# The last two attention heads' blocks in turns, and three orders tied around the end of the last QKV slab

## The chip, the cores and the metric

The kernel runs on one NeuronCore of a Trainium2 chip. The metric is the device time of one execution in microseconds, the median of repeated runs. Five engines work side by side, each through its own queue in order: PE (TensorE) multiplies into PSUM, DVE (VectorE), ACT (ScalarE) and POOL (GpSimd) work elementwise, and SP (SyncE) issues most DMAs. Line numbers (L823) are those of the kernel before.

## The reference

A decoder trunk of two layers on 512 tokens of width 1024, all in float32. Layer 0 has a convolution module, layer 1 differential attention; each is followed by a SwiGLU FFN and a gated input embedding. The change touches layer 1 alone, from its QKV product to its output product:

```python
qkv = x @ w_qkv                              # 1024 x 3072
q, k = rms_norm(q), rms_norm(k)              # per head, two components of 64
for each block of 128 queries, 8 heads, 2 components:
    probs = softmax(q @ k.T + bias, causal)
    w = probs[0] - lam * probs[1]
    o = w @ v                                # v 128 wide per head
o = rms_norm(o) * (1 - lambda_init)
h = h + o.reshape(S, 1024) @ w_o
...
h = h + sigmoid(rms_norm(h) @ ple_w_gate) * (p @ ple_w_proj)   # after the FFN
```

## The kernel before, in words

**Products.** A float32 product is three passes (`mm3`, L158 to L160): each operand is split into a high and a low part. A weight arrives by a DMA on SP's queue (`wraw`, two buffers), ACT copies its high part (L151), DVE subtracts the low part (L153; POOL does one split in each slab but the first).

**QKV in slabs.** Six slabs of 512 columns follow each other (`QKV`): q and k of heads 0 and 1, v of heads 0 to 3, q and k of heads 2/3, of 4/5, v of heads 4 to 7, q and k of heads 6/7. A slab has four token blocks (`tokens`), each a chain of 24 passes on PE. For a q/k slab, `unit` then copies the product to `q`, squares it on ACT, reduces it on DVE (L765), takes the power on POOL (L766, L767), scales on POOL (L769); `unit_end` transposes on PE (L775) and splits into the parts that the scores use: ACT (L783, L784), POOL (L788), DVE (L791, L793).

**Attention blocks.** A block is a head and 128 queries, (hd, qb), hd and qb from 0. `stage_s` makes two scores on PE (L820, L821; 128 to 512 keys wide by qb), reduces each against the bias on DVE (L823), takes the exponential on ACT (L827) and combines both on DVE (L830 to L832). `stage_t`, two blocks later, transposes on PE (L840) and copies on ACT (L842). `stage_a`, four blocks later, multiplies by v on PE (L853), and when a head is full scales it (L861, L871 to L876). `stage_o` transposes a finished head on PE (L883) and splits it (L182 on ACT, L183 on DVE). Scores have two PSUM buffers (`sc`), transposes two (`tp`).

**Their order.** `todo` lists the 32 blocks by head. The last number of each entry of `QKV` says how many blocks' stages are traced between the products of each token block, so 25 of the 32 blocks go into the slabs. What is left is taken one piece at a time by `step()`: first in `project`, the eight products with `ple_w_proj` that the gate needs at the end of the layer (48 passes, weights `pw`), then in `linear` with W_o. W_o's first two columns of tiles (m = 0, 1) run together, k by k, each k needing one finished head. The trace order is not the queue order: a scheduler places each instruction in its engine's queue by simulated times; `tc.issue_after(ins)` ties an instruction behind another one of its engine.

Of the kernel before, what the change touches and what calls it, by code (L numbers as in the profile page):

```python
# [24 lines left out]
NH = 8  # L25
# [47 lines left out]
HALVES = slice(0, DH), slice(DH, P)  # L73
LT = 2
LA = 4
SQ_ACT = True
PACK = True
E1 = True
GLO = 1
QKV = (("q", 0, (0, 0, 0, 0)), ("v", 0, (1, 1, 1, 2)), ("q", 1, (1, 1, 1, 2)), ("q", 2, (1, 1, 2, 1)), ("v", 1, (1, 1, 2, 2)), ("q", 3, (1, 1, 1, 1)))  # L80


@with_exitstack
def trunk(ctx, tc, xT, pT, wts, diag, dww, vec, rel, onehot, lamv, out):
# [9 lines left out]
    def sb(shape, tag, bufs, dt=F32):  # L94
        uid[0] += 1
        return pool.tile(shape, dt, tag=tag, name=f"{tag}_{uid[0]}", bufs=bufs)
# [65 lines left out]
    def wpart(w, k):  # L162
        return tuple(t[:, k * P : (k + 1) * P] for t in w)
# [115 lines left out]

    last_product = [None]  # L280

    def project(ph, m, w, o, step=lambda: None):

        acc = mm()
        for k in range(2):
            last_product[0] = mm3(acc, wpart(w, 2 * (m % 4) + k), ph[k], k == 0, k == 1)
            step()
        last_copy[0] = A.copy(o, acc)
        return o
# [457 lines left out]
    def unit(pair, ws, tb, between):  # L747

        if tb == 0:
            qk[pair] = [sb([P, 2, S], f"C{i}", 2, F32R) for i in range(6)]  # L750

            for c in range(2):
                with tc.issue_after(n2.last.ins):
                    G.memset(f(qk[pair][4 + c][HALVES[1 - c]]), 0.0)
        acc, r = tokens(ws, tb, between)
        q = big()
        A.activation(q, acc, AF.Copy, scale=r)
        sq = wk()
        if SQ_ACT:
            A.activation(sq, acc, AF.Square, scale=r)  # L760
        else:
            G.tensor_tensor(sq, q, q, ALU.mult)

        rs = sb([P, P // 2], "r8", 2)[:, :8]
        V.tensor_reduce(out=rs, in_=sq.rearrange("p (g d) -> p g d", g=8), op=ALU.add, axis=AX.X)  # L765
        G.tensor_tensor(rs, rs, meps, ALU.add)  # L766
        G.tensor_tensor(rs, rs, mhalf, ALU.pow)  # L767
        q3 = q.rearrange("p (g d) -> p g d", g=8)
        G.tensor_tensor(q3, q3, rs.unsqueeze(2).to_broadcast([P, 8, DH]), ALU.mult)  # L769
        return pair, tb, q  # L770

    def unit_end(pair, tb, q):
        t = tp()
        for i in range(4):
            T.transpose(t[:, i * P : (i + 1) * P], q[:, i * P : (i + 1) * P], ident)  # L775
        t4 = t.rearrange("p (h c t) -> p h c t", h=2, c=2)
        cut = slice(tb * P, (tb + 1) * P)
        qs, ks, kl = qk[pair][0:2], qk[pair][2:4], qk[pair][4:6]

        qg, kg = col("q_g"), gains[:, 0:1]  # L780
        for c in range(2):
            own, other = HALVES[c], HALVES[1 - c]
            A.activation(qs[c][own, :, cut], t4[own, :, 0], AF.Copy, scale=qg[own])  # L783
            A.activation(ks[c][own, :, cut], t4[own, :, 1], AF.Copy, scale=kg[own])  # L784
            if KDUP == "A":
                A.activation(ks[c][other, :, cut], t4[own, :, 1], AF.Copy, scale=kg[own])
            else:
                G.tensor_copy(ks[c][other, :, cut], f(ks[c][own, :, cut]))  # L788
        for c in range(2):
            own, other = HALVES[c], HALVES[1 - c]  # L790
            V.scalar_tensor_tensor(  # L791
                qs[c][other, :, cut], t4[own, :, 0], qg[own], f(qs[c][own, :, cut]), ALU.mult, ALU.subtract)
            V.scalar_tensor_tensor(  # L793
                kl[c][own, :, cut], t4[own, :, 1], kg[own], f(ks[c][own, :, cut]), ALU.mult, ALU.subtract)

    biases = {}
    stats = {}
    state = {}

    def stage_s(hd, qb):  # L800
        if qb == 0:
            biases[hd] = bias(hd)
        b = biases[hd]
        n = (qb + 1) * P
        brev = bass.AP(b.tensor, b.offset + (S - 1) - (S - n), [list(b.ap[0]), [-1, n]])
        qs, ks, kl = qk[hd // 2][0:2], qk[hd // 2][2:4], qk[hd // 2][4:6]
        i = hd % 2
        if qb == 0:
            stats[hd] = sb([P, 4, 6], "st", 2)
        es, st = [], stats[hd][:, qb]  # L810
        for c in range(2):
            cut = slice(qb * P, (qb + 1) * P)
            if not PACK or n > S // 2:
                acc = sc()
            elif c == 0:
                both = sc()
                acc = both[:, : S // 2]
            else:
                acc = both[:, S // 2 :]
            T.matmul(acc[:, :n], qs[c][:, i, cut], ks[c][:, i, 0:n], start=True, stop=False)  # L820
            T.matmul(acc[:, :n], qs[c][:, i, cut], kl[c][:, i, 0:n], start=False, stop=True)  # L821
            e = sb([P, S], ("acc", "rb")[qb % 2], 1) if c and E1 else big()
            V.tensor_tensor_reduce(  # L823
                out=e[:, :n], in0=acc[:, :n], in1=brev, scale=-1.0, scalar=3.0e38,
                op0=ALU.add, op1=ALU.min, accum_out=st[:, c : c + 1],
            )
            A.activation(e[:, :n], e[:, :n], AF.Exp, scale=-1.0, bias=st[:, c : c + 1], accum_out=st[:, 2 + c : 3 + c])  # L827
            es.append(e)

        V.reciprocal(st[:, 4:5], st[:, 3:4])  # L830
        V.scalar_tensor_tensor(st[:, 5:6], st[:, 4:5], mlam, st[:, 2:3], ALU.mult, ALU.mult)
        V.scalar_tensor_tensor(es[0][:, :n], es[1][:, :n], st[:, 5:6], es[0][:, :n], ALU.mult, ALU.add)  # L832
        state[hd, qb] = es[0]

    def stage_t(hd, qb):
        w_ = state[hd, qb]
        n = (qb + 1) * P
        t = tp()
        for k in range(qb + 1):
            T.transpose(t[:, k * P : (k + 1) * P], w_[:, k * P : (k + 1) * P], ident)  # L840
        wt_ = sb([P, S], ("wth", "wtl")[qb % 2], 2)
        A.copy(wt_[:, :n], t[:, :n])  # L842
        state[hd, qb] = wt_

    oacc = {}
    osb = {}

    def stage_a(hd, qb):
        if qb == 0:
            oacc[hd] = mm()  # L850
        own = slice(qb * P, (qb + 1) * P)
        for k in range(qb + 1):
            T.matmul(  # L853
                oacc[hd][:, own], state[hd, qb][:, k * P : (k + 1) * P],
                val[hd // 4, k // 2][:, k % 2, (hd % 4) * P : (hd % 4 + 1) * P], start=(k == 0), stop=(k == qb),
            )
        if qb % 2 == 1:
            if qb == 1:
                osb[hd] = sb([P, S], f"D{hd % 6}", 1)
            two = slice((qb - 1) * P, (qb + 1) * P)  # L860
            V.tensor_copy(osb[hd][:, two], oacc[hd][:, two])  # L861
        if qb == 3:
            o_ = osb[hd]

            rs = sb([P, P // 2], "r8", 2)[:, :8]
            e0 = sb([P, 4], "r0", 1)
            A.activation(e0, stats[hd][:, :, 2], AF.Square, scale=math.sqrt(P * EPS))
            sq = wk()
            for k in range(4):
                cut = slice(k * P, (k + 1) * P)  # L870
                A.activation(sq[:, cut], o_[:, cut], AF.Square, accum_out=rs[:, k : k + 1])  # L871
            G.tensor_tensor(rs[:, 0:4], rs[:, 0:4], e0, ALU.add)
            G.tensor_tensor(rs[:, 0:4], rs[:, 0:4], mhalf[:, 0:4], ALU.pow)
            rs = rs[:, 0:4]
            o3 = o_.rearrange("p (g d) -> p g d", g=4)
            G.tensor_tensor(o3, o3, rs.unsqueeze(2).to_broadcast([P, 4, P]), ALU.mult)  # L876

    ot = {}

# [7 lines left out]
        ot[hd] = (hi, lo)  # L887


    todo = [(hd, qb) for hd in range(NH) for qb in range(4)]  # L890
    stages = []
    for n in range(len(todo) + LA):
        for stage, at in ((stage_s, n), (stage_a, n - LA), (stage_t, n - LT)):
# [13 lines left out]
    for what, at, pace in QKV:  # L907
        ws = slab(GLO if at > 0 else 0)
        for tb in range(4):
# [10 lines left out]
            if (what, at, tb) == ("q", 0, 1):  # L920
                ph = pfeatures(1, [both(sb([P, 2, S], t, 1, F32R)) for t in ("B4", "B5")])
            elif (what, at, tb) == ("q", 0, 2):
                pw = [weight(parts=("B6", "B7"))]
    unit_end(*waiting)
    pw.append(weight())


    done = [0]
# [1 line left out]
    def step():  # L930
        if stages:
            n, s = stages.pop(0)
            s()
        else:
            n = 99
        while done[0] < NH and (n - LA - 3) // 4 > done[0]:
            stage_o(done[0])
            done[0] += 1

    pp = []  # L940
    for m in range(NC):
        if m % 2 == 0:
            o2 = sb([P, 2, S], f"C{m // 2 + 2}", 2)
        step()
        pp.append(project(ph, m, pw[m // 4], o2[:, m % 2], step))

    def heads_until(k):
        while done[0] <= k:
# [5 lines left out]
        V.tensor_tensor(h[m], acc, h[m], ALU.add)  # L954
        norm.chunk(m)

    linear(NC, ot, add_attn, 2, heads_until, step, parts={4: ("B0", "B1"), 5: ("B2", "B3")})
    n2 = Norm("ple_g1")
    ffn(norm, n2)

# [133 lines left out]
```

## Time and profile before

| | |
|---|---|
| median of 3 runs | 1285.97 us (1285.86 to 1286.89) |
| the profiled execution, its own time | 1286.35 us |
| its span | 1284.6 us |
| granted PE clock, mean | 0.999 |
| the last q/k slab and what follows to W_o's second pair of tiles | about 757 to 850 us of the span |

The span is what the trace shows; 1.75 us of the profiled execution's own time lie outside it. Times in the views are microseconds from the span's start.

### The profile page before, as it was taken

Reading aid. Unit: us, or ns where it says so; the run is one execution under the profiler, and the core shown is the slowest. Engines: PE = TensorE matmul, PEld = TensorE weight load, DVE = VectorE, ACT = ScalarE, POOL = GpSimd, SP = SyncE. Lnnn points to the kernel's source line nnn. Section 1 sums busy time; section 2 is a strip of 40 time slices with the busy share of each in tenths; the row PEclk is TensorE's granted clock in tenths of the full one; section 3 lists DMA queues with packets and bytes.
Section 4 is the critical chain, followed back from the end, with each engine's and each line's share of the span. In section 5 each row is a group of like instructions: output and inputs, shape, how many; then the busy total and the mean of one; then the engine's idle time right before and its main releaser. Section 6 shows DMA issues by size and latency. Waiting matters only on the chain.

```text
span 1284.6 us, 15478 instructions
## 1 busy us (share of the span) xinstructions
PE 1267.4 (99%) x5960; PEld 1051.5 (82%) x5960; DVE 707.2 (55%) x1040; ACT 523.3 (41%) x874; POOL 247.4 (19%) x223
## 2 busy tenths in 40 slices
PE   9999999999999999999999998999999999999998
PEld 8888688888888888888888887878888888888887
DVE  4897765543344434456677777536443344334445
ACT  5752464332222223254567768635321223222332
POOL 1754432000000000042346546131000000000030
PEclk9999999999999999999999999999999999999999
DMA  7555214223333333233342222022332222232231
GB/s 269 198 179 179 83 52 126 88 96 99 98 98 98 99 93 94 67 126 99 97 128 77 74 83 75 33 82 82 99 98 98 98 98 92 91 97 91 91 115 66
DMA packets 46838, 131.97 MB, mean 103 GB/s; under 512 B 5379, under 2 KB 9987, under 8 KB 46764
## 3 DMA queue, kind: packets, MB, share of 16 engines
q1 hardware_dynamic: 44640, 127.55, 31.1%
q10 hardware_dynamic: 2124, 3.43, 0.9%
q8 instruction: 47, 0.77, 0.3%
q14 instruction: 27, 0.22, 0.1%
HBM read 126.75 MB, written 4.21 MB: 102 GB/s over the span
## 4 chain that ended last, share of the span: by engine, by line
PE 81%; DVE 7%; DMA 4%; issue 3%; POOL 2%; ACT 2%; SPq 0%; ACTq 0%; DVEq 0%; POOLq 0%
PE mm L158 26%; PE mm L159 26%; PE mm L160 26%; DVE sc L421 2%; DVE wlo L153 2%; POOL wk L409 1%; DMA wraw<-in_wts 1%; PE mm L853 1%; ACT whi L151 1%; DMA po<-big 1%; PE sc L821 1%; PE sc L820 1%; PE tp L840 1%; DMA B<-po 0%; ACT A L182 0%
## 5 line engine op out<-in xcount | busy, mean ns | idle before, releaser
L151 ACT CAST whi<-wraw 128x1024 fp32r<-128x1024 f32 (+2 forms) x210 | 214.2, 1026 | 549.3 <-PE mm L160 356.4
L158 PE MATMUL mm<-A,wlo 128*128 128x512 f32 (+1 forms) x1080 | 420.8, 390 | 1.8 <-ACT A L182 1.8
L159 PE MATMUL mm<-A,whi 128*128 128x512 f32 (+1 forms) x1080 | 419.2, 388 | 0.0
L160 PE MATMUL mm<-A,whi 128*128 128x512 f32 (+1 forms) x1080 | 415.8, 389 | 0.0
L153 DVE TENSOR_TENSOR wlo<-wraw,whi 128x1024 fp32r<-128x1024 f32 (+2 forms) x206 | 257.6, 1254 | 88.3 <-ACT whi L151 87.9
L158 PEld LDWEIGHTS mm<-A,wlo 128*128 128x128 f32 x1080 | 202.8, 188 | 44.7 <-ACT A L182 2.4
L159 PEld LDWEIGHTS mm<-A,whi 128*128 128x128 f32 x1080 | 202.8, 188 | 42.1 <-issue 1.2
L160 PEld LDWEIGHTS mm<-A,whi 128*128 128x128 f32 x1080 | 202.7, 188 | 41.8 <-issue 0.5
L206 POOL TENSOR_TENSOR acc<-acc,wk 128x512 f32<-128x512 f32 x35 | 57.4, 1640 | 772.0 <-issue 660.0
L158 PE MATMUL mm<-B,wlo 128*128 128x512 f32 x360 | 141.2, 392 | 0.0
L160 PE MATMUL mm<-B,whi 128*128 128x512 f32 x360 | 140.7, 391 | 0.0
L159 PE MATMUL mm<-B,whi 128*128 128x512 f32 x360 | 140.6, 390 | 0.0
L637 DVE TENSOR_TENSOR h<-mm,h 128x512 f32<-128x512 f32 x48 | 33.0, 691 | 123.3 <-PE mm L160 123.3
L629 DVE TENSOR_TENSOR big<-mm,rb 128x512 f32<-128x512 f32 x44 | 30.4, 691 | 126.4 <-PE mm L160 126.4
L627 DVE TENSOR_TENSOR big<-mm,rb 128x512 f32<-128x512 f32 x44 | 30.4, 691 | 99.5 <-PE mm L160 92.7
L160 PEld LDWEIGHTS mm<-B,whi 128*128 128x128 f32 x360 | 67.6, 188 | 14.8
L159 PEld LDWEIGHTS mm<-B,whi 128*128 128x128 f32 x360 | 67.6, 188 | 14.5
L158 PEld LDWEIGHTS mm<-B,wlo 128*128 128x128 f32 x360 | 67.6, 188 | 14.4
L158 PE MATMUL mm<-whi,A 128*128 128x512 f32 x192 | 76.1, 398 | 0.0
L159 PE MATMUL mm<-whi,A 128*128 128x512 f32 x192 | 75.6, 395 | 0.0
L160 PE MATMUL mm<-wlo,A 128*128 128x512 f32 x192 | 74.9, 398 | 0.1
L409 POOL TENSOR_TENSOR wk<-wk,C 128x512 f32<-128x512 f32 x35 | 51.9, 1483 | 24.2 <-ACT C L408 19.3
(211 smaller groups left out, 1359.4 us busy)
## 6 DMA issues: line engine op xcount, KB each, us to landing
wraw<-in_wts SPq DMA_DIRECT2D x193, 512.0 KB, 3.5
wraw<-in_wts SPq DMA_DIRECT2D x16, 384.0 KB, 3.0
D<-in_diag SPq DMA_DIRECT2D x22, 256.0 KB, 4.3
C<-in_diag SPq DMA_DIRECT2D x16, 256.0 KB, 4.7
h<-in_xT SPq DMA_DIRECT2D x8, 256.0 KB, 5.4
bias<-scr ACTq DMA_DIRECT2D x8, 256.0 KB, 3.4
out_t<-h SPq DMA_DIRECT2D x7, 256.0 KB, 2.0
wraw<-in_wts SPq DMA_DIRECT2D x4, 256.0 KB, 4.1
```

What stands on the lines that cost most here:

```text
L151: A.copy(hi[:, cut], raw[:, cut])
L153: eng.tensor_tensor(lo[:, cut], raw[:, cut], f(hi[:, cut]), ALU.subtract)
L158: T.matmul(acc, al, bh, start=first, stop=False)
L159: T.matmul(acc, ah, bh, start=False, stop=False)
L160: return T.matmul(acc, ah, bl, start=False, stop=last)
L206: self.last = self.eng.tensor_tensor(self.acc, self.acc, sq, ALU.add)
L409: G.tensor_tensor(pacc, pacc, pr, ALU.add)
L421: last_v_tap[0] = V.scalar_tensor_tensor(sum_, tap(j), wt(c, j), sum_, ALU.mult, ALU.add)
L627: V.tensor_tensor(tg, pg, rb, ALU.mult)
L629: V.tensor_tensor(tu, pu, rb, ALU.mult)
L637: V.tensor_tensor(h[m], acc, h[m], ALU.add)
L820: T.matmul(acc[:, :n], qs[c][:, i, cut], ks[c][:, i, 0:n], start=True, stop=False)
```

## The change

1. **Pace.** The slabs take 5, 5, 6, 6, 6 blocks (before 5, 5, 5, 6, 4): 28 of 32.
2. **Turns.** The blocks of heads 6 and 7 alternate: (6,0), (7,0), (6,1), (7,1), ... `step` asks for a head's `stage_o` by its place in `todo`. The statistics get a third buffer.
3. **Square first.** In `unit`, ACT squares the product before it copies it.
4. **The second projection weight** is loaded and split in the second token block of the last slab, into buffers of its own (B0, B1), and no longer behind the slab.
5. **W_o's splits held.** Those of tiles 0 and 1 stand behind the last unit's splits on ACT and DVE, those of 2 to 5 behind the last block's last instructions there.
6. **The gate's products tied.** From the fourth on, a product of `project` may not be queued ahead of the last PE instruction of the step three before it.

```diff
-QKV = (... ("q", 1, (1, 1, 1, 2)), ("q", 2, (1, 1, 2, 1)), ("v", 1, (1, 1, 2, 2)), ("q", 3, (1, 1, 1, 1)))
+QKV = (... ("q", 1, (1, 1, 1, 2)), ("q", 2, (1, 2, 2, 1)), ("v", 1, (1, 1, 2, 2)), ("q", 3, (1, 1, 2, 2)))

-    def project(ph, m, w, o, step=lambda: None):
+    def project(ph, m, w, o, step=lambda: None, behind=()):
         acc = mm()
         for k in range(2):
-            last_product[0] = mm3(acc, wpart(w, 2 * (m % 4) + k), ph[k], k == 0, k == 1)
+            with tc.issue_after(behind[-3].ins) if len(behind) > 2 else nullcontext():
+                last_product[0] = mm3(acc, wpart(w, 2 * (m % 4) + k), ph[k], k == 0, k == 1)
             step()

-        q = big()
+        q, sq = big(), wk()
+        A.activation(sq, acc, AF.Square, scale=r)
         A.activation(q, acc, AF.Copy, scale=r)
-        sq = wk()
-        if SQ_ACT:
-            A.activation(sq, acc, AF.Square, scale=r)
...
     def unit_end(pair, tb, q):
...
-            A.activation(ks[c][own, :, cut], t4[own, :, 1], AF.Copy, scale=kg[own])
+            late[1] = A.activation(ks[c][own, :, cut], t4[own, :, 1], AF.Copy, scale=kg[own])
...
-            V.scalar_tensor_tensor(
+            late[0] = V.scalar_tensor_tensor(
                 kl[c][own, :, cut], t4[own, :, 1], kg[own], f(ks[c][own, :, cut]), ALU.mult, ALU.subtract)
...
-            stats[hd] = sb([P, 4, 6], "st", 2)
+            stats[hd] = sb([P, 4, 6], "st", 3)
...
-        V.scalar_tensor_tensor(es[0][:, :n], es[1][:, :n], st[:, 5:6], es[0][:, :n], ALU.mult, ALU.add)
+        last_block[0] = V.scalar_tensor_tensor(es[0][:, :n], es[1][:, :n], st[:, 5:6], es[0][:, :n], ALU.mult, ALU.add)
...
-        A.copy(wt_[:, :n], t[:, :n])
+        last_block[1] = A.copy(wt_[:, :n], t[:, :n])
...
-    todo = [(hd, qb) for hd in range(NH) for qb in range(4)]
+    todo = [(hd, qb) for hd in range(NH - 2) for qb in range(4)]
+    todo += [(hd, qb) for qb in range(4) for hd in (NH - 2, NH - 1)]
...
                 pw = [weight(parts=("B6", "B7"))]
+            elif (what, at, tb) == ("q", 3, 1):
+                pw.append(weight(parts=("B0", "B1")))
     unit_end(*waiting)
-    pw.append(weight())
...
             n, s = stages.pop(0)
-            s()
+            behind.append(s())
...
-        while done[0] < NH and (n - LA - 3) // 4 > done[0]:
+        while done[0] < NH and n >= todo.index((done[0], 3)) + LA + 4:
...
-        pp.append(project(ph, m, pw[m // 4], o2[:, m % 2], step))
+        pp.append(project(ph, m, pw[m // 4], o2[:, m % 2], step, behind))
...
-    linear(NC, ot, add_attn, 2, heads_until, step, parts={4: ("B0", "B1"), 5: ("B2", "B3")})
+    order = {0: tuple(late), 1: tuple(late), 2: last_block, 3: last_block, 4: last_block, 5: last_block}
+    linear(NC, ot, add_attn, 2, heads_until, step, split=order, parts={4: ("B0", "B1"), 5: ("B2", "B3")})
```

`linear` hands `split` to `weight` as `after`, whose first entry ties the DVE part of a split (L153) and whose second ties the ACT part (L151). The stage functions now return their last PE instruction.

More of the change, by code (lines that the diff above doesn't have):

```diff
@@ L75 @@
 LA = 4
-SQ_ACT = True
 PACK = True
@@ L79 @@
 GLO = 1
-QKV = (("q", 0, (0, 0, 0, 0)), ("v", 0, (1, 1, 1, 2)), ("q", 1, (1, 1, 1, 2)), ("q", 2, (1, 1, 2, 1)), ("v", 1, (1, 1, 2, 2)), ("q", 3, (1, 1, 1, 1)))
+QKV = (("q", 0, (0, 0, 0, 0)), ("v", 0, (1, 1, 1, 2)), ("q", 1, (1, 1, 1, 2)), ("q", 2, (1, 2, 2, 1)), ("v", 1, (1, 1, 2, 2)), ("q", 3, (1, 1, 2, 2)))
 @with_exitstack
@@ L755, in unit @@
         acc, r = tokens(ws, tb, between)
-        q = big()
+        q, sq = big(), wk()
+        A.activation(sq, acc, AF.Square, scale=r)
         A.activation(q, acc, AF.Copy, scale=r)
-        sq = wk()
-        if SQ_ACT:
-            A.activation(sq, acc, AF.Square, scale=r)
-        else:
-            G.tensor_tensor(sq, q, q, ALU.mult)
         rs = sb([P, P // 2], "r8", 2)[:, :8]
@@ L770, in unit @@
         return pair, tb, q
+    late = [None, None]
     def unit_end(pair, tb, q):
@@ L792, in unit_end @@
                 qs[c][other, :, cut], t4[own, :, 0], qg[own], f(qs[c][own, :, cut]), ALU.mult, ALU.subtract)
-            V.scalar_tensor_tensor(
+            late[0] = V.scalar_tensor_tensor(
                 kl[c][own, :, cut], t4[own, :, 1], kg[own], f(ks[c][own, :, cut]), ALU.mult, ALU.subtract)
+    last_block = [None, None]
     biases = {}
@@ L820, in stage_s @@
             T.matmul(acc[:, :n], qs[c][:, i, cut], ks[c][:, i, 0:n], start=True, stop=False)
-            T.matmul(acc[:, :n], qs[c][:, i, cut], kl[c][:, i, 0:n], start=False, stop=True)
+            last = T.matmul(acc[:, :n], qs[c][:, i, cut], kl[c][:, i, 0:n], start=False, stop=True)
             e = sb([P, S], ("acc", "rb")[qb % 2], 1) if c and E1 else big()
@@ L831, in stage_s @@
         V.scalar_tensor_tensor(st[:, 5:6], st[:, 4:5], mlam, st[:, 2:3], ALU.mult, ALU.mult)
-        V.scalar_tensor_tensor(es[0][:, :n], es[1][:, :n], st[:, 5:6], es[0][:, :n], ALU.mult, ALU.add)
+        last_block[0] = V.scalar_tensor_tensor(es[0][:, :n], es[1][:, :n], st[:, 5:6], es[0][:, :n], ALU.mult, ALU.add)
         state[hd, qb] = es[0]
+        return last
     def stage_t(hd, qb):
@@ L839, in stage_t @@
         for k in range(qb + 1):
-            T.transpose(t[:, k * P : (k + 1) * P], w_[:, k * P : (k + 1) * P], ident)
+            last = T.transpose(t[:, k * P : (k + 1) * P], w_[:, k * P : (k + 1) * P], ident)
         wt_ = sb([P, S], ("wth", "wtl")[qb % 2], 2)
-        A.copy(wt_[:, :n], t[:, :n])
+        last_block[1] = A.copy(wt_[:, :n], t[:, :n])
         state[hd, qb] = wt_
+        return last
     oacc = {}
@@ L852, in stage_a @@
         for k in range(qb + 1):
-            T.matmul(
+            last = T.matmul(
                 oacc[hd][:, own], state[hd, qb][:, k * P : (k + 1) * P],
@@ L876, in stage_a @@
             G.tensor_tensor(o3, o3, rs.unsqueeze(2).to_broadcast([P, 4, P]), ALU.mult)
+        return last
     ot = {}
@@ L940, in trunk @@
     pp = []
+    behind = []
     for m in range(NC):
```

## The prediction

> **What bounds the kernel now.** I read the page's first part, then the waits of PE in the stretch of the attention layer, then the busy time by stage around the place where PE waits, and last the groups of DVE there.
>
> ```profile
> span 1284.6 us, 15478 instructions
> PE 1267.4 (99%) x5960; PEld 1051.5 (82%) x5960; DVE 707.2 (55%) x1040; ACT 523.3 (41%) x874; POOL 247.4 (19%) x223
> ```
>
> PE is busy for 1267.4 of 1284.6 us. The built programs have the same instructions on every engine (only the second projection weight's split has other buffers), so PE's work is the same to the pass, and the change can only move PE's waits. The waits of PE from 640 to 860 us (us in total, times, longest):
>
> ```profile
> PE sc L820 <- DVE C L791: 2.9, 1, 2.9
> PE tp L775 <- POOL big L769: 1.5, 2, 0.9
> PE tp L840 <- DVE A L183: 1.1, 2, 0.7
> PE mm L158 <- ACT A L182: 0.8, 1, 0.8
> PE tp L883 <- DVE A L183: 0.3, 1, 0.3
> ```
>
> They add up to 6.6 us: that, and what the clock adds, is all that there is to win. Where they lie (stretch, length, then busy time of PE, PEld, DVE, ACT, POOL, the granted clock, DMA share and rate):
>
> ```profile
> 760.00:790.00 30.00, 30.00 (x160) 25.44 (x159) 22.37 (x58) 22.45 (x63) 17.38 (x19) 1.00 0.33 95
> 797.00:800.60 3.60, 2.17 (x15) 1.57 (x13) 3.01 (x11) 2.62 (x6) 1.72 (x3) 1.00 0.35 131
> 800.60:804.00 3.40, 1.14 (x3) 0.56 (x3) 3.27 (x7) 3.33 (x10) 1.12 (x2) 1.00 0.35 89
> 804.00:807.40 3.40, 3.15 (x13) 2.51 (x13) 3.34 (x11) 2.45 (x6) 0.00 (x0) 0.50 0.17 67
> 807.40:811.00 3.60, 2.50 (x17) 1.82 (x18) 3.56 (x11) 2.24 (x5) 0.00 (x0) 0.99 0.00 0
> 846.00:851.00 5.00, 4.12 (x19) 2.99 (x18) 2.01 (x4) 1.95 (x3) 0.00 (x0) 1.00 0.00 0
> ```
>
> From 797 to 811 us, right behind the last slab, DVE is busy for 3.01 + 3.27 + 3.34 + 3.56 = 13.2 of 14.0 us. There DVE's queue is the bound and PE goes along with it; the half clock from 804.0 to 807.4 falls where DVE is busy for 3.34 of 3.40 us and so costs next to nothing itself. Up to 790 us PE has no gap worth naming. So the question is how long DVE holds PE up behind the last slab in the new order.
>
> **The change part by part.** DVE's durations there (640 to 860 us; count, busy us, mean ns):
>
> ```profile
> L153 DVE TENSOR_TENSOR wlo<-wraw,whi 128x1024 fp32r<-128x1024 f32 x23 | 35.2, 1533 | 11.3 <-ACT whi L151 11.1
> L793 DVE SCALAR_TENSOR_TENSOR C<-tp,lam,C 64x256 fp32r<-64x256 f32 x32 | 15.5, 484 | 0.6
> L765 DVE TENSOR_REDUCE r<-wk 128x8 f32<-128x512 f32 x14 | 9.5, 682 | 4.1 <-ACT wk L760 2.5 <-POOL big L769 1.1 <-ACT r L867 0.5
> L831 DVE SCALAR_TENSOR_TENSOR st<-st,lam 128x1 f32<-128x1 f32 x32 | 7.7, 241 | 0.9
> L832 DVE SCALAR_TENSOR_TENSOR big<-rb,st,big 128x512 f32<-128x512 f32 x8 | 6.8, 849 | 0.2
> L861 DVE COPY D<-mm 128x256 f32<-128x256 f32 x16 | 6.7, 420 | 5.4 <-PE mm L853 5.3
> L183 DVE SCALAR_TENSOR_TENSOR A<-tp,lam,A 128x512 fp32r<-128x512 f32 x8 | 6.0, 747 | 14.0 <-ACT A L182 14.0
> L823 DVE CUSTOM_DVE_ANT_0 big<-sc,bias 128x512 f32<-128x512 f32 x8 | 5.5, 687 | 0.7 <-PE sc L821 0.7
> L830 DVE RECIPROCAL st<-st 128x1 f32<-128x1 f32 x32 | 5.1, 160 | 8.0 <-ACT acc L827 4.3 <-ACT rb L827 3.6
> L832 DVE SCALAR_TENSOR_TENSOR big<-acc,st,big 128x384 f32<-128x384 f32 x8 | 4.9, 618 | 0.2
> L832 DVE SCALAR_TENSOR_TENSOR big<-rb,st,big 128x256 f32<-128x256 f32 x8 | 4.7, 592 | 0.1
> L823 DVE CUSTOM_DVE_ANT_0 acc<-sc,bias 128x384 f32<-128x384 f32 x8 | 4.4, 554 | 3.4 <-PE sc L821 3.4
> L823 DVE CUSTOM_DVE_ANT_0 big<-sc,bias 128x256 f32<-128x256 f32 x8 | 3.4, 420 | 0.4 <-PE sc L821 0.4
> L832 DVE SCALAR_TENSOR_TENSOR big<-acc,st,big 128x128 f32<-128x128 f32 x8 | 2.8, 352 | 0.2
> L823 DVE CUSTOM_DVE_ANT_0 acc<-sc,bias 128x128 f32<-128x128 f32 x8 | 2.3, 288 | 3.3 <-PE sc L821 3.1
> ```
>
> PE's pace is read from starts: a 512-wide pass 0.23 us, a 384-wide score pass 0.18, four transposes 0.44, eight L853 0.81.
>
> ```profile
> 817.81 0.34 PE L820 MATMUL sc<-C,C 128*128 128x384 f32 x1
> 817.99 0.34 PE L821 MATMUL sc<-C,C 128*128 128x384 f32 x1
> 819.52 0.60 PE L883 MATMUL tp<-ident,D 128*128 128x128 f32 x4
> 819.96 1.06 PE L853 MATMUL mm<-B,wtl 128*128 128x128 f32 x8
> 820.77 0.48 PE L820 MATMUL sc<-C,C 128*128 128x512 f32 x1
> 822.46 0.39 PE L159 MATMUL mm<-B,whi 128*128 128x512 f32 x1
> 822.69 0.39 PE L160 MATMUL mm<-B,whi 128*128 128x512 f32 x1
> ```
>
> A pass that is 0.39 long starts every 0.23, so each wait above is some 0.16 short of what it costs against the pace.
>
> *What goes.* From 797 to 811 us PE does at full pace five groups of stage_o transposes and the last unit's (6 x 0.44), four 384-wide score passes (0.70), four 512-wide (0.92), a 128-wide and a 256-wide pair (about 0.4) and five single transposes (0.55): 5.2 us. The stretch loses 14.0 - 5.2 = 8.8 us. The 0.8 at W_o (846 to 851 us: ACT's split of the last head) and the 0.9 of an earlier unit, one of the two waits of L775 behind POOL, make 1.0 and 1.1 more. In the new order both go: head 7's transposes stand behind 36 passes of W_o's first pair instead of between the last ones, and the earlier unit's transposes stand later on PE. Gone: 10.9 us.
>
> *What comes.* The built queues behind the last slab read, on PE: scores and transposes of the first blocks of heads 6 and 7, then the last unit's transposes, the scores of (6,2), (7,2), (6,3), (7,3) with the stage_o transposes of heads 0 to 4 between them, and only then six of the eight tied products. So the work that filled PE before is now queued behind the stretch that DVE bounds.
> (a) The transposes of (6,0) wait for its combine. From its second score DVE has L823, two unit splits, L765, L861, L830, the next L823, L831 and L832: 0.29 + 0.97 + 0.68 + 0.42 + 0.16 + 0.42 + 0.24 + 0.35 = 3.5 us. PE has one pass, eight L853 and three pairs of narrow scores: 1.7. Wait 1.8. For (7,0) DVE has three L823 (1.1), two L830 and L831 (0.8), L832 of 256 and 128 (0.9) = 2.9, PE 1.5: wait 1.4. Together 3.2 us.
> (b) From the third unit's splits to the split of head 3, DVE has eight unit splits (3.9), four L823 of 384 (2.2), two of 512 (1.4), four L183 (3.0), a L830, L831 and L832 (1.0), and W_o's two held splits, which stand just here: at 1.23 each (the last row below, not the mean of 1.53) 2.5. Sum 13.9; neighbours overlap by up to 0.09, so 13.2. PE has 1.4 + 1.84 for the scores and 5 x 0.44: 5.4. Wait 7.8 us.
> (c) The transposes of (6,3) wait for head 5's split in the second buffer: about 0.8, as L840 behind L183 above.
> Came: 11.8 us. Net +0.9.
>
> ```profile
> 799.32 1.05 ACT L151 CAST B<-wraw 128x1024 fp32r<-128x1024 f32 x1 [0.96 <-DMA wraw<-in_wts]
> 800.39 1.23 DVE L153 TENSOR_TENSOR B<-wraw,B 128x1024 fp32r<-128x1024 f32 x1
> ```
>
> *The held splits* wait behind the last unit; behind them on ACT stand the exponentials of the last two heads, on DVE the reduction of (7,2), and for these PE waits: priced in (b). Those of tiles 2 to 5 stand behind the last block, beside W_o's first 48 passes (10.9 us): cover enough for 2 x (1.05 + 1.23) at nothing, 2.3 if it were gone. *The projection weight* leaves 799.3 to 801.6 us (0.96 + 1.05 on ACT, 1.23 on DVE: this takes the 2.9 us wait apart) for the last slab, where 760 to 790 us shows PE full and DVE with 7.6 us free: nothing, 1.2 if that is not so. SP's queue keeps its order and POOL gets no more. *The extra blocks in the slabs* bring DVE about 2 us each there (two L823, L830 to L832) under the same cover. *Square first* takes 0.7 of ACT off a chain that PE covers. The third statistics buffer costs nothing.
>
> *The clock.* Half clock was granted in the 3.4 us after a stretch with PE busy for 1.14 of 3.40 us. In (b) PE works 5.4 of 13.2 us, so such stretches come again; inside (b) they are hidden by DVE, but the last may reach into the dense products behind: between 0 and 1.7 us (half of 3.4). I take 0.4, nearer to nothing since most of it lies inside. [...]
>
> The sum: +0.9 + 0.4 = +1.3 us on the profiled execution's own 1286.35: 1287.65; that execution lies 0.38 over the median of the runs, so **1287.3 us**.
>
> **The rivals.** *Faster.* The turns give each head's chain the other head's scores to hide behind, and DVE's queue may drain sooner than its sum. If (a) is hidden (-3.2) and W_o's splits fall beside ACT's exponentials instead of adding to DVE's line (-2.5 of (b)), 1287.3 - 5.7 = 1281.6 us. It decides once the waits that come are below 8 us. Against it: DVE was busy for 13.2 of 14.0 us in the same place before, and nothing is taken off it but 1.2 us, with 2.5 put on. *Slower.* DVE's line in (b) at its slow durations: L153 at its mean 1.53 (+0.6), L832 and POOL's scaling holding each other up at the last unit's end, as here (+0.7 on the 0.85 of L832, +1.1 on POOL's usual 1.0), and the half clock's full 1.7 in the products (+1.3).
>
> ```profile
> 786.67 2.12 POOL L769 TENSOR_TENSOR big<-big,r 128x512 f32<-128x512 f32 x1
> 787.81 1.53 DVE L832 SCALAR_TENSOR_TENSOR big<-rb,st,big 128x512 f32<-128x512 f32 x1
> 796.89 1.04 POOL L769 TENSOR_TENSOR big<-big,r 128x512 f32<-128x512 f32 x1
> ```
>
> That is +3.7: 1291.0 us. It decides as soon as (b) loses 1.3 us more than summed. For it: the last unit's POOL chain runs beside the combines of (6,1) and (7,0). *Nothing changes.* DVE's whole line behind the slab is the same instructions, so the loss is only moved: 10.9 for 10.9 gives 1286.0 us; this lies in the forecast's own range.
>
> **How the numbers follow.** A measurement of this kernel can tell about 0.2%, 2.6 us, from no change: faster is under 1283.4, slower over 1288.5. The forecast with "nothing changes" gets 0.52, its own range 1284.8 to 1288.5 (the clock's 0, and 2 us of error either way in waits of some 11 us each). The slower rival gets 0.34, since most unknown costs point that way, the faster one 0.14. The range of 8 in 10 reaches up to nearly all of the slower rival, 1290.6, and down to 1284.0, leaving out most of the faster one.
>
> **What would show it.** Right: DVE busy for over 90% in some 13 us behind the last slab, with W_o's L153 in it; PE waits for L832 before two transposes; no 2.9 us wait on L791; no wait on L182 at W_o. Wrong: PE busy for over 80% of that stretch (then the faster rival), the granted clock half beyond the last L823 (then the slower one), or waits of PE within the slabs, which I put at nothing.

## The result

The changed kernel takes 1289.68 us (median of 20 runs, 1287.15 to 1292.21), where the kernel before took 1286.90 in the runs made beside it (20 runs, 1284.15 to 1289.82): a ratio of 1.0021, with a 95% interval of 1.0013 to 1.0029. That is 2.7 us slower (1.7 to 3.7). The prediction was 1.3 us slower, with a range from 1284.0 to 1290.6. The profiled execution took 1287.56 us, below that median. First the head of its page. (From here on a line number is that of the view beside it. In the changed kernel's views L819 to L822 are the lines L820 to L823 of before, L829 to L831 are L830 to L832, L885 is L883, the last unit's transposes L773 and splits L789 and L791 are L775, L791 and L793, and the splits L152 and L182 are L153 and L183.)

```profile
span 1285.8 us, 15470 instructions
PE 1269.6 (99%) x5960; PEld 1052.9 (82%) x5960; DVE 708.1 (55%) x1040; ACT 523.1 (41%) x874; POOL 243.6 (19%) x223
```

PE's work is the same to the pass, as expected, so its queues can be laid over each other. The spans of the two profiled executions differ by only 1.2 us, because the kernel before lost some 2.4 us early, far from the change, in this one execution. Two points of PE's queue that are the same in both show it: the last unit transposes before the attention blocks move, and a pass of W_o's products, first for the kernel before, then for the changed one. The transposes are four in both; the views end within the group.

```profile
649.28 0.49 PE L775 MATMUL tp<-ident,big 128*128 128x128 f32 x3
885.13 0.39 PE L159 MATMUL mm<-A,whi 128*128 128x512 f32 x1
```

```profile
646.85 0.38 PE L773 MATMUL tp<-ident,big 128*128 128x128 f32 x2
886.34 0.39 PE L158 MATMUL mm<-A,whi 128*128 128x512 f32 x1
```

Between them lie 235.85 us before and 239.49 us after: 3.6 us more in this pair of executions, 2.7 in the ratio of all runs. The waits of PE in the changed kernel from 640 to 860 us:

```profile
PE sc L819 <- DVE st L830: 1.8, 1, 1.8
PE tp L885 <- DVE C L791: 1.5, 1, 1.5
PE tp L840 <- DVE big L831: 1.3, 1, 1.3
PE sc L819 <- DVE st L822: 1.3, 2, 1.1
PE sc L819 <- DVE C L789: 1.2, 2, 1.1
PE tp L885 <- DVE st L829: 0.6, 1, 0.6
```

Of the waits of before those behind POOL (1.5), at W_o (0.8) and behind the splits of finished heads (1.1 and 0.3) are gone. That of the scores on the last unit's split is not gone but down from 2.9 to 1.2 (L791 before, L789 here). The others, all on DVE too, are new. The changed kernel in stretches of 3.4 us (columns as in the prediction's table):

```profile
790.00:793.40 3.40, 1.37 (x9) 0.83 (x7) 3.15 (x13) 1.81 (x10) 1.91 (x3) 0.96 0.01 2
793.40:796.80 3.40, 2.80 (x9) 2.21 (x9) 2.72 (x9) 1.96 (x7) 3.14 (x4) 0.54 0.00 0
796.80:800.20 3.40, 2.28 (x14) 1.73 (x14) 1.78 (x7) 2.31 (x7) 0.39 (x1) 1.00 0.01 2
800.20:803.60 3.40, 2.50 (x10) 1.46 (x10) 3.20 (x8) 3.34 (x6) 1.19 (x3) 1.00 0.00 0
803.60:807.00 3.40, 1.13 (x6) 0.72 (x6) 3.34 (x9) 2.90 (x7) 0.00 (x0) 0.97 0.00 0
807.00:810.40 3.40, 2.58 (x9) 1.92 (x10) 3.37 (x10) 0.97 (x3) 0.00 (x0) 0.50 0.72 173
810.40:813.80 3.40, 3.40 (x13) 2.55 (x12) 3.36 (x11) 3.40 (x10) 0.00 (x0) 0.53 0.34 135
813.80:817.20 3.40, 3.27 (x21) 2.53 (x19) 3.40 (x9) 2.41 (x7) 0.00 (x0) 1.00 0.00 0
```

From 800.2 to 813.8 us DVE is busy for 13.27 of 13.60 us. The half clock is granted in three of these stretches, for some 10 us in all, where the kernel before had it in one, for 3.4 us.

### The profile page after: what moved, and what is told of

It is laid out like the page before. It is cut to its first block, busy times and chain, and to the rows that moved or that the text cites. A ratio compares the mean times of both kernels' runs of the same rounds, so it can differ in the third digit from the quotient of the medians.

```text
span 1285.8 us, 15470 instructions
## 1 busy us (share of the span) xinstructions
PE 1269.6 (99%) x5960; PEld 1052.9 (82%) x5960; DVE 708.1 (55%) x1040; ACT 523.1 (41%) x874; POOL 243.6 (19%) x223
## 4 chain that ended last, share of the span: by engine, by line
PE 85%; DVE 6%; DMA 3%; issue 2%; POOL 2%; ACT 2%; SPq 0%; DVEq 0%; POOLq 0%; ACTq 0%
PE mm L157 27%; PE mm L159 27%; PE mm L158 27%; DVE sc L421 2%; POOL wk L409 2%; DVE wlo L152 1%; PE mm L854 1%; DMA wraw<-in_wts 1%; DMA po<-big 1%; PE tp L840 1%; PE sc L819 1%; PE sc L820 1%; PE tp L773 0%; ACT whi L150 0%; ACT A L181 0%
## 5 line engine op out<-in xcount | busy, mean ns | idle before, releaser
L152 DVE TENSOR_TENSOR wlo<-wraw,whi 128x1024 fp32r<-128x1024 f32 (+2 forms) x205 | 255.6, 1250 | 91.0 <-ACT whi L150 90.9
L157 PE MATMUL mm<-B,wlo 128*128 128x512 f32 x352 | 137.8, 391 | 0.0
L158 PE MATMUL mm<-B,whi 128*128 128x512 f32 x352 | 137.4, 390 | 0.0
L159 PE MATMUL mm<-B,whi 128*128 128x512 f32 x352 | 137.4, 390 | 0.0
L159 PEld LDWEIGHTS mm<-B,whi 128*128 128x128 f32 x352 | 66.1, 188 | 14.5
L158 PEld LDWEIGHTS mm<-B,whi 128*128 128x128 f32 x352 | 66.0, 188 | 14.3
```

The costliest lines, as they stand in the source:

```text
L152: eng.tensor_tensor(lo[:, cut], raw[:, cut], f(hi[:, cut]), ALU.subtract)
L157: T.matmul(acc, al, bh, start=first, stop=False)
L158: T.matmul(acc, ah, bh, start=False, stop=False)
L159: return T.matmul(acc, ah, bl, start=False, stop=last)
```

## The experiments

Ratios are to the kernel before, run on the same chip beside each experiment. Each "edit" starts from the changed kernel. The theories in short: the loss comes from the **ties** of the gate's products, from W_o's **held splits**, or from the **turns** themselves.

**No ties.**

```
-        pp.append(project(ph, m, pw[m // 4], o2[:, m % 2], step, behind))
+        pp.append(project(ph, m, pw[m // 4], o2[:, m % 2], step))
```

> The change without the ties of gate's products to the steps (nothing else altered). Theory ties: the products that the ties hold back, 36 passes at 0.23 us = 8.3 us of TensorE work, are missing in the stretch where VectorE bounds; free, they stand among the last two units' transposes and the scores and fill its waits (in the trace of the changed kernel the waits of TensorE there sum to 7.7 us). Expected 5 to 8 us under the changed kernel, so a ratio to the kernel before of 0.996 to 0.999, and waits of TensorE in the stretch under 3 us in all. Theory held splits: VectorE's line behind the slab is as long as it was, the products only change places, and the time stays within 1 us of the changed kernel (ratio 1.001 to 1.003). Theory turns: as held splits, since the order of the blocks stays.

Measured: 1282.26 us, ratio 0.9967 (0.9956 to 0.9979). That is 6.9 us under the changed kernel ((1.0021 - 0.9967) x 1286), and 4.2 us under the kernel before. Waits of PE, 640 to 870 us:

```profile
PE sc L819 <- DVE st L830: 1.8, 1, 1.8
PE mm L157 <- DVE wlo L152: 0.8, 1, 0.8
PE tp L840 <- DVE big L831: 0.3, 1, 0.3
PE tp L885 <- DVE C L791: 0.2, 1, 0.2
PE sc L819 <- DVE st L822: 0.2, 1, 0.2
```

What fills the stretch is seen when PE's passes from 790 to 814 us are grouped by line. First the changed kernel, then the one without ties; mm<-B,B are the gate's products:

```profile
L157 PE MATMUL mm<-B,B 128*128 128x512 f32 x2 | 1.3, 626 | 0.0
L158 PE MATMUL mm<-B,B 128*128 128x512 f32 x2 | 1.0, 512 | 0.0
L159 PE MATMUL mm<-B,B 128*128 128x512 f32 x2 | 1.0, 510 | 0.0
```

```profile
L157 PE MATMUL mm<-B,B 128*128 128x512 f32 x16 | 7.0, 435 | 0.0
L159 PE MATMUL mm<-B,B 128*128 128x512 f32 x16 | 6.8, 427 | 0.0
L158 PE MATMUL mm<-B,B 128*128 128x512 f32 x16 | 6.8, 422 | 0.0
```

6 passes with ties, 48 without. By the code all passes but the six of the first product are tied, 42 of 48; in the changed kernel 36 of them start behind the stretch, from 814.14 us on. DVE's line is no shorter without ties: from the third unit's splits to the split of head 3 it takes 14.1 us (802.30 to 816.38) where it took 13.2, and W_o's two splits still stand in it. But PE now works beside it.

**Ties further back.** The distance of the tie was changed, and with it the number of steps that must be there before a product is tied; so fewer products are tied, too. For fifteen back the numbers are 15 and 14.

```
-            with tc.issue_after(behind[-3].ins) if len(behind) > 2 else nullcontext():
+            with tc.issue_after(behind[-9].ins) if len(behind) > 8 else nullcontext():
```

> The whole change, but a product waits for the ninth step back instead of the third. Theory ties with the pace (the loss is the work that the ties keep out of the stretch where VectorE bounds): 12 more passes stand ahead of the last scores, 12 x 0.23 = 2.8 us less waiting: ratio 0.999 to 1.001 where the change has 1.0021. Theory any tie (a tie of whatever distance breaks the planner's filling): as the change, 1.001 to 1.003.

> The whole change, but a product waits for the fifteenth step back. By the theory of the work kept out, all but three of the tied passes stand in the stretch, and W_o's first passes follow: the ratio goes down to that without ties, 0.996 to 0.998. By the theory of any tie it stays over 0.999.

Measured: nine back 0.9997 (0.9988 to 1.0006), fifteen back 0.9982 (0.9971 to 0.9992). The same grouping, 790 to 814 us, nine back and then fifteen back:

```profile
L159 PE MATMUL mm<-B,B 128*128 128x512 f32 x7 | 2.8, 403 | 0.0
L157 PE MATMUL mm<-B,B 128*128 128x512 f32 x6 | 2.6, 436 | 0.0
L158 PE MATMUL mm<-B,B 128*128 128x512 f32 x6 | 2.4, 395 | 0.0
```

```profile
L157 PE MATMUL mm<-B,B 128*128 128x512 f32 x13 | 6.2, 477 | 0.0
L159 PE MATMUL mm<-B,B 128*128 128x512 f32 x13 | 6.0, 463 | 0.0
L158 PE MATMUL mm<-B,B 128*128 128x512 f32 x13 | 6.0, 460 | 0.0
```

So 6, 19, 39 and 48 passes in the stretch go with ratios of 1.0021, 0.9997, 0.9982 and 0.9967. From one end to the other that is 6.9 us for 42 passes, 0.16 us a pass, where a pass costs 0.23 us in a full queue. So at this pace a tie as such does no harm; the work that it keeps out of the stretch does. (Fifteen back stays just above the 0.996 to 0.998 expected of it.) The half clock doesn't explain these times: in the four profiled executions it was granted behind the slab for 10.2, 3.4, 6.8 and 3.4 us in the same order, while the times only fall.

**The old pace, with ties and without.**

```
-("q", 2, (1, 2, 2, 1)) ... ("q", 3, (1, 1, 2, 2))
+("q", 2, (1, 1, 2, 1)) ... ("q", 3, (1, 1, 1, 1))
```

> The change with the pace of before: two blocks fewer in the slabs, two more behind them; ties, turns and held splits stay. Theory ties: a product is tied to the step three back, so with more steps left behind the slab the products stand earlier among them, and TensorE's waits shrink: 2 to 5 us under the changed kernel, ratio 0.998 to 1.000. Theory pace (the blocks moved into the slabs are the gain of the change, and something else loses it): VectorE gets two blocks, 4 us, more behind the slab: 2 to 4 us over the changed kernel, ratio 1.004 to 1.005.

> The change without ties and with the pace of before: turns and held splits stay. Theory pace (two more blocks in the slabs take 4 us of VectorE's line from behind the slab, where it bounds): 2 to 4 us over the kernel with the pace and no ties, ratio 0.998 to 1.000. Theory turns (the gain is theirs alone): ratio 0.996 to 0.9975.

Measured: with ties 0.9977 (0.9966 to 0.9987), without 0.9974 (0.9961 to 0.9987). With the old pace the ties cost nothing that can be measured; with the new pace they cost 6.9 us. With ties the result is far from the theory of pace and just under the range of the theory of ties; without, it is that of the theory of turns. The pace by itself, without ties, goes from 0.9974 to 0.9967, well inside the intervals. (The slabs take 25 blocks at the old pace and 28 at the new: three blocks move, not two as the expectations say.)

Why the ties cost nothing here is seen in where the gate's products stand. With ties and without, 27 of their passes are counted between 790 and 814 us, and not one starts between 796 and 807 us. There DVE bounds: from 796.8 to 807 us it is busy for 9.72 of 10.2 us with ties and for 9.50 without. At the new pace 3 passes start between 796 and 807 us with the tie to the third step back, 12 with the ninth, 22 with the fifteenth and 30 without ties. So at the old pace the ties have nothing to keep out: the scheduler, left free, doesn't put the products there either. Why it does so at one pace and not at the other these runs don't show, nor why the old pace is about as fast without that filling. The count of passes orders the times at the new pace only.

**The old order, with ties and without.** Turns undone as here, pace undone as above, splits held:

```
-    todo = [(hd, qb) for hd in range(NH - 2) for qb in range(4)]
-    todo += [(hd, qb) for qb in range(4) for hd in (NH - 2, NH - 1)]
+    todo = [(hd, qb) for hd in range(NH) for qb in range(4)]
```

> The change without turns and pace: the ties stand on the order of blocks of before (held splits stay). Beside the same kernel without ties (held splits only) it prices the ties where more steps are left behind the slab. Theory ties alone (the tie costs whatever the order): 5 us or more over that kernel. Theory ties with turns and pace (a product waits for the third step back, and the turns and the pace put that step behind the last unit's transposes and all the scores): with two blocks more behind the slab the products stand among the scores, and the ties cost 0 to 2 us.

> The change without ties, turns and pace: what stays is W_o's splits held, the second projection weight's earlier place and the square first. It asks where the gain comes from that the change has once the ties are gone (ratio 0.9967). Theory turns and pace (the gain is theirs): products c and d stand ahead of the last unit's transposes as in the kernel before, and the stretch behind the slab has none to fill it; the time is within 1.3 us of the kernel before, ratio 0.999 to 1.001. Theory splits and weight (the gain is that the conversions of weights leave the place where VectorE bounds): 3 to 5 us faster, ratio 0.996 to 0.998.

Measured: with ties 0.9995 (0.9986 to 1.0005), without 0.9994 (0.9983 to 1.0004). Here too the ties cost nothing, and none of the gate's passes starts between 796 and 807 us in either. The gain of the version without ties is not there either: held splits, the weight's earlier place and the square first are together within 0.2% of the kernel before. With the turns added it is 0.9974: the turns bring some 2.6 us ((0.9994 - 0.9974) x 1286), though the two intervals overlap (0.9961 to 0.9987 and 0.9983 to 1.0004); the two kernels, run beside each other, took 1285.11 and 1281.64 us. For turns undone under the new pace there is no time: the last slab would then already take blocks of head 6 that read projections not yet written.

**No held splits, with ties and without.**

```
-    linear(NC, ot, add_attn, 2, heads_until, step, split=order, parts=...)
+    linear(NC, ot, add_attn, 2, heads_until, step, parts=...)
```

> The change without W_o's splits held (no order of the splits given); ties, turns and pace stay. Theory held splits: the two VectorE splits of 1.22 us each leave the line behind the last slab, 2.5 us under the changed kernel: ratio 0.999 to 1.000. Theory ties: VectorE's line may shorten, but PE still has nothing to do beside it; 0 to 2.5 us under the changed kernel, ratio 0.9995 to 1.002, TensorE's waits in the stretch still over 5 us.

> The change without ties and without held splits: turns and pace stay. Theory turns and pace: the gain stays whole, ratio 0.996 to 0.998, since the products fill the stretch wherever the splits stand. Theory splits: W_o's two splits stand ahead of the last unit's transposes on VectorE and ScalarE and hold them up by up to 2.5 us on VectorE and 2 us on ScalarE: 2 us or more over the kernel with the splits held and no ties, ratio 0.998 to 1.000.

Measured: with ties 1.0020 (1.0008 to 1.0032), the same as the changed kernel. That is against the theory of held splits and as the theory of ties has it, with waits of PE that add up to 7.1 us; without ties 0.9983 (0.9973 to 0.9994), in the range of the theory of splits, with an interval that reaches into that of turns and pace. Let free, the two splits stand earlier in DVE's line, ahead of the reduction of a narrow score that PE's next scores wait for. Without ties and hold, from DVE's and then PE's timeline:

```profile
793.63 1.23 DVE L152 TENSOR_TENSOR wlo<-wraw,whi 128x1024 fp32r<-128x1024 f32 x1
795.82 0.41 DVE L822 CUSTOM_DVE_ANT_0 big<-sc,bias 128x256 f32<-128x256 f32 x1
796.16 1.22 DVE L152 TENSOR_TENSOR wlo<-wraw,whi 128x1024 fp32r<-128x1024 f32 x1
```

```profile
796.39 0.55 PE L819 MATMUL sc<-C,C 128*128 128x256 f32 x1 [3.00 <-POOL r L762]
```

The wait is put down to POOL's small operation, but the scores start 0.2 us after the DVE reduction at 795.82 to 796.23 that followed the first split. The wait was 1.8 us with the splits held. Holding them is worth about 2 us without ties ((0.9983 - 0.9967) x 1286), nothing with them; the intervals overlap.

**Head 5's scaling taken off POOL**, to see what DVE's long pair is:

```
+            if hd == 5:
+                for g in range(4):
+                    A.activation(o3[:, g], o3[:, g], AF.Copy, scale=rs[:, g : g + 1])
+            else:
-            G.tensor_tensor(o3, o3, rs.unsqueeze(2)...)
+                G.tensor_tensor(o3, o3, rs.unsqueeze(2)...)
```

> The whole change, but the output scaling of head 5 (POOL L877, 1.04 us) is done by ScalarE in four parts of 0.3 us. In the trace of the changed kernel two VectorE operations L830 of some 0.22 us each take 2.07 us while POOL runs L877 and L765 one behind the other. Theory lock (VectorE is held until POOL's operation ends): POOL's two operations become one, VectorE's pair takes 1.0 us less, the transposes of (7,0) wait 1.0 us less, and the time falls by 0.5 to 1.0 us (ratio 1.0013 to 1.0018). Theory chance (the 2.07 us have another cause): the pair stays near 2 us.

Measured: 1.0013 (1.0002 to 1.0024), 1.0 us under the changed kernel in the middle and not told apart from it by the interval. The timeline tells more. The changed kernel, then this one:

```profile
794.64 2.07 DVE L830 SCALAR_TENSOR_TENSOR st<-st,lam 128x1 f32<-128x1 f32 x2
794.66 1.04 POOL L877 TENSOR_TENSOR D<-D,r 128x512 f32<-128x512 f32 x1
795.65 1.04 POOL L765 TENSOR_TENSOR big<-big,r 128x512 f32<-128x512 f32 x1
796.63 0.47 DVE L831 SCALAR_TENSOR_TENSOR big<-rb,st,big 128x256 f32<-128x256 f32 x1
```

```profile
795.21 0.34 DVE L830 SCALAR_TENSOR_TENSOR st<-st,lam 128x1 f32<-128x1 f32 x2
795.75 1.09 POOL L765 TENSOR_TENSOR big<-big,r 128x512 f32<-128x512 f32 x1 [0.37 <-ACT big L758]
795.86 1.13 DVE L831 SCALAR_TENSOR_TENSOR big<-acc,st,big 128x128 f32<-128x128 f32 x1
```

The pair falls from 2.07 to 0.34 us, and the remaining POOL operation now holds an L831 instead (1.13 us, 0.34 at its usual). From the pair's start to the end of both L831 DVE needs 2.73 us in the changed kernel (794.64 to 797.37) and 1.78 here (795.21 to 796.99). PE's transposes of (6,0) and of (7,0), which wait for this, first in the changed kernel, then here:

```profile
792.79 0.30 PE L840 MATMUL tp<-ident,big 128*128 128x128 f32 x1
797.51 0.30 PE L840 MATMUL tp<-ident,big 128*128 128x128 f32 x1 [1.31 <-DVE big L831]
```

```profile
793.59 0.30 PE L840 MATMUL tp<-ident,big 128*128 128x128 f32 x1
797.13 0.30 PE L840 MATMUL tp<-ident,big 128*128 128x128 f32 x1 [1.41 <-DVE big L831]
```

The listed wait does not fall by 1.0 us, as was expected: it is 1.4 here and 1.3 before. But from one group to the other PE takes 3.54 us instead of 4.72. Here the granted clock is 1.00 from 790 to 800.2 us, where the changed kernel had 0.50 from 793.14 to 796.56 us. PE's own work between the groups ends sooner (the last score starts 1.85 us behind the first group, 793.59 to 795.44, instead of 2.99, 792.79 to 795.78), and more of the time counts as waiting.

**The third W_o tile's split held less far back**, without ties:

```
-    order = {..., 2: last_block, ...}
+    order = {..., 2: tuple(late), ...}
```

> The change without ties, and the split of W_o's third tile held behind the last unit as the first two are, not behind the last block. Without ties W_o's first passes fill the stretch and no longer cover that split: there TensorE waits 0.8 us for VectorE's L152 ahead of the third tile. Theory cover gone: that wait goes, 0.8 to 1.1 us less, ratio 0.9955 to 0.997 where without ties alone it was 0.9967. If VectorE's line, now 1.2 us longer behind the slab, bounds again: 1 us more, 0.997 to 0.998.

Measured: 1282.65 us, 0.9967 (0.9955 to 0.9979): no gain that can be measured. In the trace the 0.8 us wait of the third tile is gone; the time doesn't show it, though it repeats the result of the version without ties, 4.2 us faster than before.

## Why the prediction was right or wrong

*The outcome.* The sign was right, the size (+1.3) was under the measured +2.7, which lies just past the bound of 0.2% that I took for "slower", between the forecast and the slower rival (+5.0) and nearer to the forecast.

*What goes.* Right but for one: the waits on POOL and at W_o are gone; that on L791 of before fell from 2.9 to 1.2 us.

*(a), the first transposes of heads 6 and 7.* The listed waits, 1.8 and 1.3 us, look like the sum's 1.8 and 1.4, but that is luck. The first stands one place earlier, at the second score of (6,1), and the second is short because PE ran at half the clock there (0.50 from 793.14 to 796.56 us; passes of 512 started 0.42 us apart, 794.72 and 795.14, where the pace is 0.23). Measured against the pace, as the sum was, PE takes 4.1 us (788.67 to 792.79) to the transposes of (6,0) for its 1.7 us of work, and from there 4.7 us (to 797.51) for 1.5: it loses 2.4 and 3.2 us, together 5.6 where the sum has 3.2. Mis-sized above all is the second. I had counted DVE's queue at its usual durations, 2.9 us; in truth 4.7 us lie between the ends of the two combines (792.64 to 797.37), and POOL's hold on the pair of L830 is 1.7 of them. The slower rival had named this (POOL and DVE holding each other up at the last unit's end) and priced it at 1.8, with the hold on the combine instead.

*(b), the stretch that DVE bounds.* From the third unit's splits to the split of head 3 I summed 13.2 us of DVE's line. It was 13.17:

```profile
800.22 0.48 DVE L789 SCALAR_TENSOR_TENSOR C<-tp,vec,C 64x256 fp32r<-64x256 f32 x1 [0.64 <-ACT C L782]
805.37 1.22 DVE L152 TENSOR_TENSOR wlo<-wraw,whi 128x1024 fp32r<-128x1024 f32 x1
806.98 1.22 DVE L152 TENSOR_TENSOR wlo<-wraw,whi 128x1024 fp32r<-128x1024 f32 x1
812.64 0.75 DVE L182 SCALAR_TENSOR_TENSOR A<-tp,lam,A 128x512 fp32r<-128x512 f32 x1
```

PE takes 13.2 us there as well (800.84 to 814.00) for its 5.4 us of work, a loss of 7.7 to 7.8 where the sum has 7.8.

```profile
800.84 0.41 PE L819 MATMUL sc<-C,C 128*128 128x384 f32 x1 [1.05 <-DVE C L789]
814.00 0.38 PE L840 MATMUL tp<-ident,big 128*128 128x128 f32 x2
```

*Between (a) and (b)* stands a term that I left out: DVE itself waits, for ACT's exponential and for ACT's part of the last unit (the 0.64 above), and PE's next scores wait for DVE's split (the 1.05 above). From 797.51 to 800.84 us PE has 1.9 us of work in 3.3 and loses 1.4.

*(c)*: 0.8 expected, no such wait in the list.

*The whole.* Read from this one execution the stretch loses 5.6 + 1.4 + 7.7 = 14.7 us, where I had 11.8 and 0.4 for the clock. Less the 10.9 that went, that makes 3.8 us, against the 3.6 that lie between the two executions and the 2.7 of all runs. Two terms were too small by 3.8 us in all, and (c) and the clock's 0.4 did not come; that the forecast came as near as it did is partly luck.

*The held splits* were charged 2.5 in (b), and they do stand there at 1.22 each. But that is no cost of holding them: free, they stand earlier and cost as much (ratio 1.0020 without the hold).

*The clock*: 0.4 expected, for stretches that come again. There were 10 us of half clock against 3.4. At 793.4 to 796.8 us PE was busy for 2.80 us at a granted clock of 0.54 (about 1.5 at full clock, by my estimate from these two numbers), but the transposes behind it waited for DVE anyway; at 807 to 813.8 DVE was busy for 6.73 of 6.80 us. The last half clock ended at 813.6 us, ahead of the dense products that the 0.4 was for (from 814.14 on). How much of the rest reached the end isn't settled by these runs.

*The extra blocks under the slabs' cover at nothing*: right, no wait within the slabs. But I priced the whole built order and so did not see that the ties cost only at the new pace.

*The signs.* DVE was busy for over 90% behind the slab (13.27 of 13.60 us) with W_o's splits in its line, and nothing waited at W_o. Of the two transposes that were to wait for a combine only those of (7,0) did.

*The faster rival* (waits that come below 8 us) did not happen with the ties: the listed waits do add up to 7.7, but the loss that the sum speaks of was 14.7. It did happen without them: 1282.26, near its 1281.6, though not by its mechanism. Its argument against, that nothing is taken off DVE's line, was sound for the change as a whole and beside the point for its best part: it was enough to leave PE its own work beside that line.

## What to carry to other kernels

Where one engine's line bounds a stretch, look for independent work that the other engine can do beside it. A dependency added to keep such work "for later" should be checked in the trace, after every other change that moves the work around it: the same tie ("the third step back") cost nothing that can be measured in one schedule (0.03%) and 0.54% in another. A list of waits is not the loss: an engine that runs slowly while it would have waited anyway hides part of it. Take a combined change apart before giving it up: here the rest was worth 0.33% once one of its six parts was gone.

## What the runs showed of the hardware

Half the clock was granted here without a long wait of PE. In the version without ties PE's longest wait was 1.8 us; from 790 to 796.8 us PE was still busy for only 4.77 of 6.80 us, and half the clock was granted from 796.3 to 799.7 us.

In all thirteen traces each time at half the clock behind the slab is 3.41, 6.83 or 10.24 us long. In three of them PE was busy for this much of the 3.41 us ahead of each half clock, and of one stretch as long that full clock followed:

| run | stretch | PE busy | clock behind it |
|---|---|---|---|
| changed kernel | 789.73 to 793.14 | 1.51 us | half |
| changed kernel | 803.38 to 806.79 | 1.29 us | half |
| no ties | 792.91 to 796.32 | 1.52 us | half |
| head 5's scaling on ACT | 789.69 to 793.11 | 1.62 us | full |
| head 5's scaling on ACT | 803.35 to 806.76 | 1.13 us | half |

These are readings of single executions and no border: in the old order with ties PE was busy for 1.89 of 3.00 us from 794 to 797 us, and half the clock followed from 797.2 us. No run here moves PE's share alone.

VectorE operations on 128x1 elements took about the whole length of the GpSimd operations beside them: two L830 took 1.07 us each, 2.07 together, from 794.64 us on, while POOL ran two operations of 1.04 us on 128x512 elements, from 794.66 and 795.65 us on. With head 5's scaling on ScalarE neither of these ran beside the pair, and it took 0.34 us (from 795.21 us on; POOL's L874, on 128x4 elements, ran to 795.38). There an L831 on 128x128 elements, which started 0.11 us behind POOL's operation of 795.75 to 796.84 us, took 1.13 us and ended at 796.99; in the changed kernel, with no POOL operation beside it, it took 0.34. What holds them up inside the chip no run here shows.
